# A decoder layer on one core: first-stage dummies, loads, small operations and products put at other places

## The chip, the cores and the metric

The kernel runs on one core of one Trainium2 chip. The metric is the time of one execution on the device in microseconds (us). The engines are named TensorE (PE, with its weight loads as PEld), VectorE (DVE), ScalarE (ACT), GpSimd (POOL) and SyncE (SP), whose queue issues most of the loads.

## What is computed

The reference is one layer of a conditioned decoder on 512 tokens of 1024 channels, in float32. Cut to what matters here:

```python
cs  = silu(c)                                   # c: one row of 1024
mod = cs @ w_ada + b_ada                        # six rows of 1024
shift1, scale1, gate1, shift2, scale2, gate2 = split(mod, 6)
h    = rmsnorm(x, norm1_g) * (1 + scale1) + shift1
proj = h @ w_in                                 # qa, ka, va, qd, kd, vd, ga, gd
out_a = sliding_window_attention(qa, ka, va, sinks)       # 8 heads, window 128
lam   = exp(sum(lp0 * lp1)) - exp(sum(lp2 * lp3)) + 0.2
out_d = rmsnorm(softmax_1 - lam * softmax_2 attention)    # 4 heads of two maps
merged = sigmoid(ga) * (out_a @ w_a) + sigmoid(gd) * (out_d @ w_d)
x = x + gate1 * (merged @ w_out)
x = x + gate2 * conv_ffn(rmsnorm(x, norm2_g) * (1 + scale2) + shift2)
return rmsnorm(x, final_g)
```

## The kernel before

Every product in float32 is made of three products in a faster format: a matrix is split in a high part and the low rest, and high x high, low x high and high x low are added up in PSUM. A split is a cast on ScalarE (the high part) and a subtraction on VectorE (the low part).

The change is in the **first stage**, which makes `h` (transposed, as `hTh` and `hTl`) and at the same time its products with the first 768 columns of `w_in` (`qa`, `ka`, `va`: six column blocks, in the six PSUM tiles `acc6`). It goes over eight row blocks k of 128 channels, the `GROUPS`:

- *Modulation.* The two rows `shift1` and `scale1` of block k need 1024 rows of `w_ada`, loaded as `adaw` (two loads of 512 KB, two buffers). `ac_ops` sums them up on VectorE, weighted by `cs`: eight steps in two chains, and one addition that ends in `ac`. `reduce_mod` sums `ac` over the partitions with two products on `ones` into `pa`, and `finish_mod` makes the two columns `mod` of it on VectorE.
- *h.* `x` comes in four token tiles `xn`. For each, `stat` squares it on ScalarE, and `rstd_start` and `rstd_end` make the root on VectorE and GpSimd. `normalise` scales the first 256 channels (VectorE), `turn` transposes block 0 on TensorE, `scale_x` scales the other channels (ScalarE), and `h_turn` transposes a later block. `h_tile` makes `hTh` and `hf` from the turned block and `mod` on ScalarE, and `h_low` makes `hTl` on VectorE.
- *Weights.* `w0_k` is loaded into one of four `raw` buffers; `split_hi` casts it on ScalarE (`w0h`), `split_lo` makes the low part `w0l` on VectorE in two parts (columns 0 to 511, 512 to 767).
- *Products.* `mm_k(k, part)` issues six products for each of three parts: `w0h` x `hTh`, `w0l` x `hTh`, `w0h` x `hTl`, that is all six PSUM tiles in one part before the next part.

Work runs one block ahead: while TensorE multiplies block k, VectorE sums the modulation of block k + 1. In this stage the order on VectorE, ScalarE and TensorE is that of the program text, written by hand (`manual_schedule`); the loads on SyncE's queue and whatever stands behind the stage in the text are placed by a planner, which may pull an instruction of the next stage in between.

Before the first product, TensorE has nothing to do for some time. `keep_warm(n)` gives it n products of the constants `ident` and `ones` into a PSUM tile that is overwritten later; each is two passes in the trace. In the code before there are 14 ahead of the first turn, and three behind each of the first three turns:

```python
    keep_warm(WARM)
    ac_ops(0, 0, KT)
    ...
    for t in range(NT):
        stat(t)
        if t:
            normalise(t - 1)
            turn(t - 1)
            keep_warm(3)
        if t == 1:
            finish_mod(0, reduce_mod(0))
```

Behind the stage, `evac_q` and `evac` move the six PSUM tiles out, and the products of the next weights start (`pq`, `pk`: heads of the second attention, units that `prefetch` loads and splits two ahead and that `fill` issues step by step). `ada_rows` sums the other four rows of the modulation on VectorE (`arow`) from loads `ra`, a step at a time between the products.

Of the kernel before, what the change touches and what calls it, by code (L numbers as in the profile page):

```python
# [8 lines left out]
F32 = mybir.dt.float32  # L9
# [26 lines left out]
NORM_LAG = 16  # L36
SWA_FILL = (2, 2, 5, 2, 2, 2, 2, 3)
DIFF_FILL = (3, 2, 4, 2)
WARM = 14
GROUPS = ((0,), (1,), (2,), (3,), (4,), (5,), (6,), (7,))  # L40
AC_CUT = 7
MOD_AT = 2
# [11 lines left out]
def kernel(  # L54
# [152 lines left out]
            )  # L207
        adaw[k] = aw

    load_ada(groups[0])  # L210
    for t in range(NT):
        nc.sync.dma_start(xn[:, t], xd[t * P : (t + 1) * P, :])
    for g in groups:
        if g[0]:
            load_ada(g)
        for k in g:
            r = raw_tile([P, 768], f"w0_{k}")
            nc.sync.dma_start(r, win[k * P : (k + 1) * P, 0:768])
            w0[k] = r
    nc.sync.dma_start(sink, swa_sinks[0].partition_broadcast(P))  # L220
    nc.sync.dma_start(
        lamv.rearrange("p a b -> p (a b)"), diff_lambda[0].rearrange("a b -> (a b)").partition_broadcast(P)
    )
    nc.sync.dma_start(crow[0:66, :], conv_w[0].rearrange("t (a p) -> (t a) p", p=P))
    nc.sync.dma_start(crow[66:88, :], conv_b[0].rearrange("(a p) -> a p", p=P))

    DONE = (0, 4, 2, 5, 1, 3)
    acc6 = {i: (fbank, sbank, vbank)[(0, 0, 1, 2, 1, 1)[i]](f"a{i}") for i in DONE}
# [5 lines left out]
    nc.vector.reciprocal(cs, cs)  # L234
    nc.vector.tensor_mul(cs, cs, pc8)
    pc = tbank("pc", (P, NR))
    nc.tensor.transpose(pc, rows, ident[:NR, :NR])
    cols = cpool.tile([P, NR], F32, name="cols")
    nc.vector.tensor_copy(cols, pc)
# [31 lines left out]
    def finish_mod(gi, pas):  # L271
        for k, pa in zip(groups[gi], pas):
            m = pp.tile([P, 16], F32, tag="mod", bufs=3, name=f"mod{k}")
            nc.vector.scalar_tensor_tensor(
                m[:, 0:1], pa[:, 0:1], bsc1[:, k : k + 1], n1g[:, k : k + 1], ALU.add, ALU.mult
            )
            nc.vector.tensor_add(m[:, 1:2], pa[:, 1:2], bsh[:, k : k + 1])
            mods[k] = m

    def w0_views(k):  # L280
        wh, wl = wts[k]
# [42 lines left out]
    def mm_k(k, part):  # L324
        wh, wl = wts[k]
        last = k == KT - 1
        if last and part == 2:
            return
        for i in DONE:
            for p in (1, 2) if last and part else (part,):  # L330
                lhs, rhs = ((wh, hTh), (wl, hTh), (wh, hTl))[p]
                nc.tensor.matmul(  # L332
                    acc6[i], lhs[:, i * P : (i + 1) * P], rhs[k], start=k == 0 and p == 0, stop=last and p == 2
                )


    def keep_warm(n):
        for i in range(n):
            nc.tensor.matmul(acc6[5][:, :P], ident, ones, start=True, stop=True)

    keep_warm(WARM)
    ac_ops(0, 0, KT)
    rst = pp.tile([P, NT], F32, name="rst")
    half = [None] * NT

# [17 lines left out]
    for t in range(NT):  # L363
        stat(t)
        if t:
            normalise(t - 1)
            turn(t - 1)
            keep_warm(3)
        if t == 1:
            finish_mod(0, reduce_mod(0))  # L370
    split_hi(0)
    normalise(NT - 1)
    turn(NT - 1)
    h_tile(0)
    split_lo(0, 0)
    split_lo(0, 1)
# [4 lines left out]
    for gi, g in enumerate(groups):  # L381
        nxt = groups[gi + 1] if gi + 1 < len(groups) else ()

        for k in nxt:
            split_hi(k)
        if gi == 0:
            for t in range(NT):
                scale_x(t)

        if nxt:  # L390
            ac_ops(gi + 1, 0, AC_CUT)
        h_low(g[0])
        if nxt:
            ac_ops(gi + 1, AC_CUT, KT)

        for k in g:
            if k == g[0] and len(nxt) == 1:
                h_turn(nxt[0])
            for part in range(3):
                if part == MOD_AT and k == g[-1] and nxt:  # L400
                    pas = reduce_mod(gi + 1)
                    split_lo(nxt[0], 0)
                    finish_mod(gi + 1, pas)
                    split_lo(nxt[0], 1)
                    for n in nxt[1:]:
                        split_lo(n, 0)
                        split_lo(n, 1)
                    for n in nxt:
                        if len(nxt) > 1:
                            h_turn(n)  # L410
                        h_tile(n)
                mm_k(k, part)
            if k == g[0]:
                for n in g[1:]:
                    h_low(n)
# [10 lines left out]
    def evac(hi, lo, src, scale=None):  # L426
        if scale is None:
            nc.scalar.copy(hi, src)
            nc.vector.tensor_sub(lo, src, hi.bitcast(F32))
        else:  # L430
            nc.scalar.activation(hi, src, AF.Copy, scale=scale)
            nc.vector.scalar_tensor_tensor(lo, src, scale, hi.bitcast(F32), ALU.mult, ALU.subtract)

    def evac_q(i):
        evac(qa[:, i, 0], qa[:, i, 1], acc6[i], qsc[:, i : i + 1])

    evac_q(0)
    evac(ka[:, 0], ka[:, 1], acc6[4])
    evac_q(2)
    vT = ap.tile([P, S], F32, tag="tmp", bufs=2, name="vaT")  # L440
    nc.scalar.copy(vT, acc6[5])
    evac_q(1)

    def turn_va():
        pv = tbank("pva")
# [6 lines left out]
    nc.tensor.transpose(pcv, crow, ident[:88, :88])  # L452
    cv = cpool.tile([P, P], F32, name="cv")
    nc.vector.tensor_copy(cv[:, :88], pcv)


    lp = cpool.tile([P, 2, 64], F32, name="lp")
    ls = cpool.tile([P, 2], F32, name="ls")
    nlam = cpool.tile([P, 1], F32, name="nlam")
    nc.vector.tensor_mul(lp, lamv[:, 0:4:2], lamv[:, 1:4:2])  # L460
    nc.vector.reduce_sum(ls, lp, axis=mybir.AxisListType.X)
    nc.scalar.activation(ls, ls, AF.Exp)
    nc.vector.tensor_sub(nlam, ls[:, 1:2], ls[:, 0:1])
    nc.vector.tensor_scalar_add(nlam, nlam, -LAM_INIT)
    nsink = cpool.tile([P, 8], F32, name="nsink")
    nc.vector.tensor_scalar_mul(nsink, sink, -1.0)


    def load_cols(src, col, name):
# [294 lines left out]
    def ada_rows():  # L764
        todo = [(idx, hf, k) for idx in range(4) for hf in range(2) for k in range(0, KT, 2)]
        r = ada_load(*todo[0])
        yield
        for (idx, hf, k), job in zip(todo, todo[1:] + [None]):
            nxt = ada_load(*job) if job else None
            if k == 0:  # L770
                ac = big.tile([P, S], F32, tag=("sq2", "g2b1")[hf], name=f"arow{idx}{hf}")
            with tc.high_priority(offset=HP // 2) if tick[0] > ADA_EASY else ExitStack():
                for a in range(2):
                    cc = cs[:, k + a : k + a + 1]
                    if k + a == 0:
                        nc.vector.tensor_scalar_mul(ac, r[:, a], cc)
                    else:
                        nc.vector.scalar_tensor_tensor(ac, r[:, a], cc, ac, ALU.mult, ALU.add)  # L778
            if k == KT - 2:
                after(ADA_LAG, lambda idx=idx, hf=hf, ac=ac: ada_spread(idx, hf, ac))  # L780
            r = nxt
            yield
# [46 lines left out]
    ada = ada_rows()  # L829
    add_head(0)  # L830
    add_head(1)
    fill(SWA_FILL[0])
    swa_scores(0, (0, 1))
    with tc.issue_after(pairs[0].last.ins):
# [982 lines left out]
```

## Time and profile before

| | us |
|---|---|
| median of three runs | 701.18 |
| the three runs | 700.99, 701.18, 702.16 |
| the profiled execution: its time | 702.35 |
| its span, first to last instruction | 700.5 |
| TensorE busy in the span | 682.6 |
| VectorE busy | 573.1 |
| ScalarE busy | 375.1 |
| mean granted TensorE clock | 0.995 |

Rows of the profile give the start and the duration in us, the engine, the line of the kernel (L332 is line 332), the operation, the tile that is written and those that are read, and in brackets the idle time of the engine just before and what ended it. Several like instructions in a row are one row with their count. TensorE's products overlap, so starts say more than durations.

### The profile page before, as it was taken

Reading aid. Unit: us, or ns where it says so; the run is one execution under the profiler, and the core shown is the slowest. Engines: PE = TensorE matmul, PEld = TensorE weight load, DVE = VectorE, ACT = ScalarE, POOL = GpSimd, SP = SyncE. Lnnn points to the kernel's source line nnn. Section 1 sums busy time; section 2 is a strip of 40 time slices with the busy share of each in tenths; the row PEclk is TensorE's granted clock in tenths of the full one; section 3 lists DMA queues with packets and bytes.
Section 4 is the critical chain, followed back from the end, with each engine's and each line's share of the span. In section 5 each row is a group of like instructions: output and inputs, shape, how many; then the busy total and the mean of one; then the engine's idle time right before and its main releaser. Section 6 shows DMA issues by size and latency. Waiting matters only on the chain.

```text
span 700.5 us, 11253 instructions
## 1 busy us (share of the span) xinstructions
PE 682.6 (97%) x4203; PEld 595.0 (85%) x4203; DVE 573.1 (82%) x1100; ACT 375.1 (54%) x666; POOL 82.4 (12%) x100
## 2 busy tenths in 40 slices
PE   6999999999999999999999999999999999999995
PEld 5777777777788888888889999999999999888884
DVE  5999886887985656663589999888888999979996
ACT  4646666454552333332468656655555666656664
POOL 3000000000001000000030111112111102540300
PEclk9999999999999999999999999999999999999998
DMA  9995454354535676239717788786889738997903
GB/s 313 289 273 159 149 152 151 98 173 121 140 102 160 207 232 185 91 99 281 251 39 144 151 200 199 174 209 184 209 213 217 173 129 219 191 198 196 166 1 120
DMA packets 115862, 121.81 MB, mean 174 GB/s; under 512 B 4383, under 2 KB 93280, under 8 KB 115808
## 3 DMA queue, kind: packets, MB, share of 16 engines
q1 hardware_dynamic: 96894, 95.09, 43.4%
q0 software_dynamic: 18720, 25.73, 22.0%
q8 instruction: 33, 0.54, 0.3%
q10 hardware_dynamic: 194, 0.28, 0.1%
q14 instruction: 21, 0.17, 0.1%
HBM read 118.97 MB, written 2.11 MB: 173 GB/s over the span
## 4 chain that ended last, share of the span: by engine, by line
PE 75%; DVE 13%; DMA 4%; ACT 4%; issue 2%; SPq 0%; POOL 0%; POOLq 0%; ACTq 0%
PE up L1152 26%; PE dc L1761 13%; DMA ra<-in_w_ada_dram 4%; PE a L332 3%; PE pgd L119 2%; PE oc L1208 2%; PE oc L1212 2%; PE pgd L121 2%; PE oc L1209 2%; PE pgd L120 2%; PE pga L119 2%; PE pga L121 2%; PE pga L120 2%; DVE arow L778 1%; DVE m_wlo L1097 1%
## 5 line engine op out<-in xcount | busy, mean ns | idle before, releaser
L1152 PE MATMUL up<-t,m_whi 128*128 128x256 f32 x528 | 96.2, 283 | 0.0
L1152 PEld LDWEIGHTS up<-t,m_whi 128*128 128x128 f32 x528 | 82.3, 192 | 0.0
L1152 PE MATMUL up<-t,m_wlo 128*128 128x256 f32 x264 | 74.7, 284 | 0.5 <-DVE m_wlo L1097 0.5
L1152 PE MATMUL up<-bh,p_wlo 128*128 128x256 f32 x232 | 65.6, 283 | 0.1
L1152 PE MATMUL up<-bh,p_whi 128*128 128x256 f32 x232 | 65.6, 283 | 0.0
L1152 PE MATMUL up<-bl,p_whi 128*128 128x256 f32 x232 | 65.6, 283 | 0.0
L778 DVE SCALAR_TENSOR_TENSOR arow<-ra,cs,arow 128x512 f32<-128x512 f32 x56 | 41.9, 749 | 21.0 <-DMA ra<-in_w_ada_dram 20.5
L1152 PEld LDWEIGHTS up<-t,m_wlo 128*128 128x128 f32 x264 | 50.6, 192 | 0.9 <-DVE m_wlo L1097 0.9
L1152 PEld LDWEIGHTS up<-bh,p_wlo 128*128 128x128 f32 x232 | 44.5, 192 | 0.3 <-DVE p_wlo L1097 0.3
L1152 PEld LDWEIGHTS up<-bl,p_whi 128*128 128x128 f32 x232 | 44.5, 192 | 0.0
L1152 PEld LDWEIGHTS up<-bh,p_whi 128*128 128x128 f32 x232 | 44.5, 192 | 0.0
L1065 POOL DMA_DIRECT2D s<-in_w_up_dram x21 | 27.0, 1360 | 143.1 <-DMA s<-in_w_up_dram 54.2
L1097 DVE TENSOR_TENSOR m_wlo<-s,m_whi 128x1024 fp32r<-128x1024 f32 x31 | 37.7, 1217 | 0.9 <-ACT m_whi L1093 0.9
L1093 ACT CAST m_whi<-s 128x1024 fp32r<-128x1024 f32 x31 | 32.4, 1047 | 9.6 <-DVE s L1087 6.2
L1152 PE MATMUL up<-t,p_whi 128*128 128x256 f32 x176 | 32.3, 284 | 0.5 <-DVE pairs L1192 0.5
L173 POOL TENSOR_TENSOR r<-ms,mhalf 128x1 f32<-128x1 f32 (+1 forms) x16 | 12.7, 796 | 133.1 <-DVE ms L171 74.1
L795 POOL DMA_DIRECT2D mod_rows<-row x8 | 5.1, 642 | 197.4 <-ACT row L794 197.4
L1152 PEld LDWEIGHTS up<-t,p_whi 128*128 128x128 f32 x176 | 27.4, 192 | 0.7 <-issue 0.7
L698 ACT ACTIVATE sd<-sd,dmx 128x128 f32<-128x128 f32 (+3 forms) x32 | 17.7, 557 | 19.0 <-DVE dmx L690 18.8
L1159 ACT ACTIVATE gT<-a,cv 128x512 f32<-128x512 f32 x22 | 17.7, 813 | 17.7 <-DVE a L1194 17.3
L1093 ACT CAST p_whi<-wa 128x1024 fp32r<-128x1024 f32 x18 | 18.7, 1041 | 12.0 <-PE up L1152 7.2
L1152 PE MATMUL up<-t,p_wlo 128*128 128x256 f32 x88 | 24.9, 283 | 0.0
(473 smaller groups left out, 2053.6 us busy)
## 6 DMA issues: line engine op xcount, KB each, us to landing
ra<-in_w_ada_dram SPq DMA_DIRECT2D x32, 512.0 KB, 3.9
wa<-in_w_up_dram SPq DMA_DIRECT2D x22, 512.0 KB, 4.0
s<-in_w_up_dram SPq DMA_DIRECT2D x21, 512.0 KB, 4.7
s<-in_w_up_dram POOLq DMA_DIRECT2D x21, 512.0 KB, 6.9
adaw<-in_w_ada_dram SPq DMA_DIRECT2D x16, 512.0 KB, 5.4
w<-in_w_in_dram SPq DMA_DIRECT2D x12, 512.0 KB, 3.9
a<-in_w_up_dram SPq DMA_DIRECT2D x11, 512.0 KB, 4.7
b<-in_w_down_dram SPq DMA_DIRECT2D x10, 512.0 KB, 3.8
```

What stands on the lines that cost most here:

```text
L119: nc.tensor.matmul(o, lh, rh, start=start, stop=False)
L120: nc.tensor.matmul(o, lh, rl, start=False, stop=False)
L121: nc.tensor.matmul(o, ll, rh, start=False, stop=stop)
L332: nc.tensor.matmul(acc6[i], lhs[:, i * P : (i + 1) * P], rhs[k], start=k == 0 and p == 0, stop=last and p == 2)
L698: exp = nc.scalar.activation(pm[m], pm[m], AF.Exp, bias=mx[:, m : m + 1], scale=slope, accum_out=lsum[:, m : m + 1])
L778: nc.vector.scalar_tensor_tensor(ac, r[:, a], cc, ac, ALU.mult, ALU.add)
L1065: nc.gpsimd.dma_start(dst, upblock(*blk), accum_op=ALU.add)
L1093: nc.scalar.copy(W[J, name][0], R[J, SRC[name]])
L1097: nc.vector.tensor_sub(lo, R[J, SRC[name]], hi.bitcast(F32))
L1152: nc.tensor.matmul(o[u], w[:, k, cu], b[:, k], start=name in ("p1", "m5", "p2") and k == 0 and x == 0, stop=k == 3 and x == 2, skip_group_ ...
L1159: nc.scalar.activation(grow(j), av[J][:, u], AF.Identity, bias=cv[:, 66 + j : 67 + j], scale=cv[:, 44 + j : 45 + j])
L1761: nc.tensor.matmul(bank2[u][:, sl], a[:, q, cu], b[:, q, sl], start=first_mm and x == 0, stop=last_mm and x == 2, skip_group_check=name no ...
```

## The change

- *Dummies:* 5 stand ahead of the transpose of `rows` (at about 4.8 us before), then 16 before and 8 behind the first reduction; behind the first three turns there are 3, 8 and 3, and 2 behind the last.
- *First sums of rows:* `reduce_mod(0)` is issued ahead of all turns; `finish_mod(0)` stays at its place on VectorE.
- *Loop:* `finish_mod` of the next block comes behind both parts of `split_lo`, no longer between them.
- *Products:* for all blocks but the last, `w0h` x `hTh` and `w0l` x `hTh` alternate tile by tile in part 0, and part 1 is empty. The order in the last block stays.
- *Loads:* the order of SyncE's first loads is written by hand. The loads of `sink`, `lamv` and `crow` come behind the last `adaw`.
- *Small operations:* the five on `lamv` and the one on `sink` are issued behind the last `h_low`.
- *Planner:* the splits of the first two head weights stay behind the last `mod` on VectorE, and the early `arow` sums behind the low part of `evac_q(1)`.

```diff
-WARM = 14
+WARM_EARLY = 5
+WARM = 24
...
-    load_ada(groups[0])
-    for t in range(NT):
-        nc.sync.dma_start(xn[:, t], xd[t * P : (t + 1) * P, :])
-    for g in groups:
-        if g[0]:
-            load_ada(g)
-        for k in g:
-            r = raw_tile([P, 768], f"w0_{k}")
-            nc.sync.dma_start(r, win[k * P : (k + 1) * P, 0:768])
-            w0[k] = r
-    (loads of sink, lamv, crow)
+    with tc.manual_schedule(engines={nc.sync.engine}):
+        load_ada(groups[0])
+        for t in range(NT):
+            nc.sync.dma_start(xn[:, t], xd[t * P : (t + 1) * P, :])
+        load_w0(0)
+        for k, ws in enumerate(((), (1,), (2, 3), (4, 5), (6,), (7,), (), ())):
+            if k:
+                load_ada(groups[k])
+            for n in ws:
+                load_w0(n)
+        (loads of sink, lamv, crow)
...
     pc = tbank("pc", (P, NR))
+    keep_warm(WARM_EARLY)
     nc.tensor.transpose(pc, rows, ident[:NR, :NR])
...
     def mm_k(k, part):
         wh, wl = wts[k]
         last = k == KT - 1
-        if last and part == 2:
+        if part == (2 if last else 1):
             return
         for i in DONE:
-            for p in (1, 2) if last and part else (part,):
+            for p in (1, 2) if last and part else (0, 1) if part == 0 and not last else (part,):
...
-    keep_warm(WARM)
+    keep_warm(WARM - 8)
     ac_ops(0, 0, KT)
+    pas = reduce_mod(0)
+    keep_warm(8)
...
             turn(t - 1)
-            keep_warm(3)
+            keep_warm((3, 8, 3)[t - 1])
         if t == 1:
-            finish_mod(0, reduce_mod(0))
+            finish_mod(0, pas)
     split_hi(0)
     normalise(NT - 1)
     turn(NT - 1)
+    keep_warm(2)
...
         h_low(g[0])
         if nxt:
             ac_ops(gi + 1, AC_CUT, KT)
+        else:
+            (lp, ls, its exponential on ScalarE, nsink, nlam: moved here)
...
                     pas = reduce_mod(gi + 1)
                     split_lo(nxt[0], 0)
-                    finish_mod(gi + 1, pas)
                     split_lo(nxt[0], 1)
+                    last_mod = finish_mod(gi + 1, pas)
...
-    evac_q(1)
+    read_q1 = evac_q(1)
...
-            with tc.high_priority(offset=HP // 2) if tick[0] > ADA_EASY else ExitStack():
+            with tc.high_priority(offset=HP // 2) if tick[0] > ADA_EASY else tc.issue_after(read_q1.ins):
...
     add_head(0)
     add_head(1)
+    with tc.issue_after(last_mod.ins):
+        prefetch()
     fill(SWA_FILL[0])
```

`issue_after(ins)` keeps the instructions of its block that run on the engine of `ins` behind `ins` in that engine's order; those on other engines and the loads are free.

## The prediction

> **What bounds the kernel now.** I read the page first: busy times, the 40 slices, the closing chain of waits.
>
> ```profile
> PE 682.6 (97%) x4203; PEld 595.0 (85%) x4203; DVE 573.1 (82%) x1100; ACT 375.1 (54%) x666; POOL 82.4 (12%) x100
> PE   6999999999999999999999999999999999999995
> PE 75%; DVE 13%; DMA 4%; ACT 4%; issue 2%; SPq 0%; POOL 0%; POOLq 0%; ACTq 0%
> ```
>
> TensorE is busy 97% of the span, and the only slices under 9 tenths are the first and the last. So TensorE's own queue sets the length, and what the change can win or lose lies in the first slices and in waits too short for a tenth to show. The change edits the first stage, which is what stands before the first `pq` product (about 60 us). I read that stretch in order of time. First the opening, up to the first product of input columns (L332):
>
> ```profile
> 2.40 0.24 PE L164 MATMUL pc<-ident,crow 8*128 8x8 f32 x1 [2.40 <-DMA crow<-in_c_dram]
> 4.80 0.27 PE L237 MATMUL pc<-ident,rows 25*128 25x25 f32 x1 [2.17 <-DMA rows<-in_diff_subln_g_dram]
> 5.00 6.14 PE L339 MATMUL a<-ones,ident 128*128 128x128 f32 x28
> 10.12 0.42 DVE L258 TENSOR_TENSOR ac<-ac,ac 128x256 f32<-128x256 f32 x1
> 11.73 0.37 DVE L356 TENSOR_SCALAR xn<-xn,rst 128x256 f32<-128x256 f32 x1
> 12.32 0.83 PE L339 MATMUL a<-ones,ident 128*128 128x128 f32 x6
> 12.99 0.50 PE L265 MATMUL pa<-ones,ac 128*128 128x1 f32 x4
> 13.53 0.22 DVE L274 SCALAR_TENSOR_TENSOR mod<-pa,cols 128x1 f32<-128x1 f32 x1 [1.44 <-PE pa L265]
> ...
> 14.64 0.47 PE L361 MATMUL xt<-ident,xn 128*128 128x128 f32 x1 [1.15 <-DVE ms L169]
> 14.91 1.49 PE L339 MATMUL a<-ones,ident 128*128 128x128 f32 x6
> 15.98 0.35 DVE L356 TENSOR_SCALAR xn<-xn,rst 128x256 f32<-128x256 f32 x1
> 16.25 0.68 DVE L304 TENSOR_TENSOR w0l<-w,w0h 128x512 fp32r<-128x512 f32 x1
> 16.41 1.42 PE L339 MATMUL a<-ones,ident 128*128 128x128 f32 x6
> 16.85 0.42 DVE L306 TENSOR_TENSOR w0l<-w,w0h 128x256 fp32r<-128x256 f32 x1
> 17.19 0.61 DVE L254 TENSOR_SCALAR ac<-adaw,cs 128x256 f32<-128x256 f32 x2
> 17.66 0.27 PE L361 MATMUL xt<-ident,xn 128*128 128x128 f32 x1
> 17.97 0.78 ACT L318 ACTIVATE hThA<-xt,mod 128x512 fp32r<-128x512 f32 x1 [3.50 <-PE xt L361]
> 18.80 1.42 PE L332 MATMUL a<-hThA,w0h 128*128 128x512 f32 x5 [0.43 <-ACT hThA L318]
> ```
>
> Columns are start, duration, engine, line, operation, output<-inputs, count. Three things are to be seen. The sum over rows of the first modulation weights is ready at 10.54 (10.12 + 0.42), but TensorE reaches its reduction `pa` only at 12.99, because it stands behind a turn of `xn` and three dummies; VectorE then waits 1.44 us for it, and the next `xn` scalings queue behind that wait. Second, six dummy passes take 0.83 us at 12.32 and 1.49 us at 14.91: (12.99 - 12.32) / 6 = 0.112 us a pass against (16.41 - 14.91) / 7 = 0.214 (six and a turn). The 28 passes from 5.00 hold 6.14, so nearly all of them ran at the slow pace too: it took some 5.8 us of steady work for the fast one. Third, the last `xn` tile is scaled by 16.33 (15.98 + 0.35), but its turn starts at 17.66, behind those slow dummies, and ScalarE's first `hThA` waits 3.50 us for it. The granted clock says the same:
>
> ```profile
> 10.00:15.00 5.00, 2.84 (x20) 2.56 (x19) 2.79 (x16) 4.25 (x8) 1.98 (x4) 0.92 1.09 372
> 15.00:20.00 5.00, 4.57 (x24) 4.15 (x24) 4.82 (x15) 2.03 (x4) 0.50 (x1) 0.74 1.11 364
> ```
>
> 0.92 and 0.74: half speed for about 0.8 us of the first and 2.6 of the second stretch, so about 14.2 to 17.6, after TensorE had stood idle for about 1.0 us behind 11.14 (5.00 + 6.14) and for 1.15 ahead of 14.64.
>
> Then the loop over the eight row blocks, k:
>
> ```profile
> 24.27 1.65 PE L332 MATMUL a<-hThA,w0h 128*128 128x512 f32 x6 [0.15 <-ACT hThA L318]
> 27.16 0.50 PE L265 MATMUL pa<-ones,ac 128*128 128x1 f32 x4
> 29.35 1.64 PE L332 MATMUL a<-hThA,w0h 128*128 128x512 f32 x6
> ...
> 34.66 1.65 PE L332 MATMUL a<-hThA,w0h 128*128 128x512 f32 x6
> ...
> 37.18 0.42 DVE L258 TENSOR_TENSOR ac<-ac,ac 128x256 f32<-128x256 f32 x1
> 37.52 0.69 DVE L304 TENSOR_TENSOR w0l<-w,w0h 128x512 fp32r<-128x512 f32 x1
> 37.75 0.58 PE L265 MATMUL pa<-ones,ac 128*128 128x1 f32 x4
> 38.37 0.22 DVE L274 SCALAR_TENSOR_TENSOR mod<-pa,cols 128x1 f32<-128x1 f32 x1 [0.16 <-PE pa L265]
> 38.57 0.42 DVE L306 TENSOR_TENSOR w0l<-w,w0h 128x256 fp32r<-128x256 f32 x1
> 38.90 0.61 DVE L254 TENSOR_SCALAR ac<-adaw,cs 128x256 f32<-128x256 f32 x2
> 40.03 1.64 PE L332 MATMUL a<-hThA,w0h 128*128 128x512 f32 x6
> ...
> 50.77 1.64 PE L332 MATMUL a<-hThB,w0h 128*128 128x512 f32 x6
> ...
> 55.86 1.65 PE L332 MATMUL a<-hThB,w0h 128*128 128x512 f32 x6
> ```
>
> From one k's first product to the next is 5.08 us once (24.27 to 29.35), and then 5.31, 5.37 and on average 5.36 (29.35 to 50.77 is 21.42 in four). The slow rounds are a ring of two engines. VectorE's sum `ac` starts at 37.18 and ends at 37.60; TensorE, done with its twelfth product, waits for it and does `pa` at 37.75; VectorE fills the latency with one part of `w0l` (37.52), runs dry, and takes `pa` up at 38.37 after 0.16 us of waiting, and only then does the other part of `w0l` (38.57) and the next seven `ac` steps. In the round of 5.08 `pa` (27.16) waits for nothing. Both engines are nearly full and each waits once for the other.
>
> **The change, part by part.**
>
> *Order in the loop.* Both parts of `w0l` now stand ahead of `mod`. From the first part to `mod` is 0.85 us now (37.52 to 38.37). The two parts back to back take 0.60 (16.25 to 16.85), and the second part to what follows 0.33 (38.57 to 38.90); the 0.33 was in the round before too. So VectorE's round goes from 5.36 to 5.36 - 0.85 + 0.60 = 5.11, or a little less without the small operations below. `pa` is then back before `mod` is reached: 0.85 after the first part against 0.93, so that wait goes. TensorE's own round without the wait is 5.08. What is late next is the two together, about 5.09: neither has more to give. Four rounds give 21.42 - 4 x 5.09 = 1.06; the sixth (50.77 to 55.86, no turns in it) loses the same wait of about 0.27. Sum: **-1.3 us**. `mod` comes 0.1 later after `ac`, so `hThA` does too; by the rows it is there at about 39.5 (38.37 + 0.22, a short `shift` step, 0.78) for products at 40.03, so 0.5 of slack covers that; without it the round would be 0.1 longer.
>
> *The products in another order* (high and low weight parts alternating per bank). The count stays at 18 a round and each has its own weight load as before, so I cost it at nothing. It asks for `w0l` at the second product instead of the seventh; in the loop that part is ready over 1 us early (38.57 + 0.42 = 38.99 against 40.03), at the start by 17.27 (16.85 + 0.42) against a second product near 18.
>
> *The opening.* `pa` of block 0 moves ahead of the turns, behind 5 and 16 dummies, and 8 + 3 + 8 + 3 dummies stand between it and the last turn. A dummy is two passes. The first five fill the idle stretch from 2.64 (2.40 + 0.24) to 4.80, so steady work starts there, and with the same 5.8 us the fast pace would come at about 8.4. Of the 32 passes from 5.0 on, 16 are then slow (3.4) and 16 fast (1.8): they end near 10.2, ahead of the sum at 10.54. `pa` then starts at 10.7 (0.15 behind the sum's end, as at 37.60 to 37.75) and takes 0.45. Then 44 passes at 0.112 are 4.93 and four turns some 0.5, so the last turn begins near 16.5, still behind its data: that was ready by 16.33 at the latest, and is earlier now without the 1.44 of waiting. `hThA` follows 0.31 behind (17.66 to 17.97): 16.8 for 17.97. I take **-1.1**. The next product block follows at the same distance, since ScalarE's queue (`hThA`, `hf`, a cast, four scalings of `xn`) sets it; VectorE's old times already suffice: `ac` of block 1 starts at 17.19 or earlier.
>
> With the clock at half for all 44 passes they take 9.4 us and `hThA` comes at 21.3, +3.3. These are the two ends. I take the fast one: the trace lost the clock after two pauses of 1.05 and 1.15 us within about 3.4, and the new order leaves one of at most about 0.7.
>
> The Trainium skill speaks against this part: "TensorE: Matmul & The Clock Gate", in "Why this matters for your kernels", asks only for no idle gaps over about 3 us, so pauses of 1.1 us would cost no clock and filling them would bring nothing. The trace disagrees: 0.74 granted behind such pauses. Part 1 of that page in the Trainium skill adds that the window in which activity is counted runs free, so the loss would vary from run to run; no single trace shows that.
>
> *Loads at fixed places.* They are issued in the order the trace already shows, except `sink`, `lamv` and the two `crow` loads, which go behind the last two blocks of modulation weights.
>
> ```profile
> 38.22 1.63 SPq L221 DMA_DIRECT2D lamv<-in_diff_lambda_dram  x1
> 39.90 0.38 SPq L224 DMA_DIRECT2D crow<-in_conv_w_dram  x1
> 42.51 1.02 SPq L205 DMA_DIRECT2D adaw<-in_w_ada_dram  x2
> 43.63 6.50 SPq L471 DMA_DIRECT2D w<-in_w_in_dram  x3
> ```
>
> That puts about 2.8 us of issue (1.63, and some 0.4 for each of three small ones) between 43.53 and the head weights now issued at 43.63, less the 0.75 by which three shorter rounds free the last slot sooner: they go 2.0 later. If their casts stand ahead of the last `hThB` in ScalarE's queue, as much of this as is not hidden stops TensorE: between 0 and 2.0 us. I take 0, as the moved loads are small and the transfers behind them start with emptier queues. The new ordering behind the last `mod` and behind `read_q1` binds only VectorE's instructions, which ran there already.
>
> *Small operations* (`lp`, `ls`, `nlam`, `nsink`) go behind the last `h_low`, where VectorE has no next block to sum: that hides them, and VectorE's rounds lose them. If `nlam` waits there for ScalarE's exponential, the splits of the head weights and the low parts of `qa` queue behind it, tenths of a us; TensorE then still has the twelve products of the last block.
>
> **The sum.** -1.3 - 1.1 = -2.4. The profiled execution took 702.35 (span 700.5 and 1.85 around it), so it would take 699.95. The median of the runs is 1.17 lower, and so is the spread between them (700.99 to 702.16): either the profile costs that much, then the sum gives 698.8, or those runs had a better opening, and then it stays near 699.9. I take 699.0. TensorE is busy in every later slice, so a shift at 58 us carries to the end. About 0.2%, 1.4 us, is what a measurement of this kernel can tell from no change.
>
> **The rivals.**
>
> *Only the loop gains* (18 in 100): the runs behind the median already have a good opening, or the pauses were not what slowed the dummies, so filling them brings nothing. By the rule of the Trainium skill's page the trace would have shown no slow passes at 14.91; it does. For the rival: the spread of 1.17. Against: the 3.50 us wait of `hThA` on the turn. 701.18 - 1.3 = 699.9, within 0.2%.
>
> *Only the opening gains* (10): the rounds stay near 5.36 because something else arrives as late, such as `hThA` behind the later `mod`, or the casts of late head weights hold ScalarE by over half of the 2.0. Against: the round of 5.08. 701.18 - 1.1 = 700.1, within 0.2%.
>
> *Slower* (10): the dummies themselves become the bound. They now stand on the path to the last turn, and each pass at half clock costs 0.1 more. 11 slow passes of the 44 eat the opening's gain, 24 the loop's as well; all of them cost 3.3 where 1.1 was gained: 701.18 + 3.3 - 1.3 = 703.2. For it: the trace shows 28 passes in a row at half clock, and a clock that fell after pauses of about 1 us. Against: from 2.6 us on there is hardly a pause left.
>
> *It does not do what it says*: the rest of the loads' order is the old one already, so that part alone would be 701.2; it is within the cases above.
>
> **How the numbers follow.** The forecast has 62 in 100, with its own range 697.6 to 699.8: -3.6 if the usual opening of the runs before has ten slow passes more than the profiled one (10 x 0.1, and the sum's 2.4), -1.4 with somewhat over half of each gain. The range of 8 in 10 reaches up over the two partial cases: 697.4 to 701.0, leaving out the slower one and the far tail of the forecast. Faster by over 0.2% (below 699.8) is the forecast's 62 and a few of the first partial case: 0.65; within 0.2% 0.25; slower 0.10.
>
> **What would show it.** Right: passes of 0.112 from about 8 us to the first product, granted clock 1.00 from 10 to 20, `pa` of block 0 near 10.7 without VectorE waiting, first product near 17.7, rounds of 5.1 and no wait of `mod` for `pa`; the first `pq` product near 57.7. Wrong: passes of 0.21 between `pa` and the last turn, rounds that stay above 5.3, ScalarE waiting for a head weight before the last `hThB`, or new waits of TensorE after 58 us.

## The result, and the profile after

The changed kernel took 700.33 us (median of 21 runs, 699.39 to 701.76); the kernel before, on the same chip, 701.80 (21 runs, 700.86 to 703.55). The ratio is 0.998, with a 95% interval of 0.9975 to 0.9986: 1.47 us faster, where the sum said 2.4 and the forecast, from the median given, 2.2. It lies inside the range (697.4 to 701.0) and half a microsecond above the likeliest case's own (up to 699.8). The profiled execution took 699.39 (span 697.5), the fastest of its 21; the profiled one of before (702.35) was half a microsecond slower than its median. So the two traces differ by 2.96 us, twice what the medians do, and must not be read as the typical pair.

The page of the changed kernel, busy times and TensorE's slices:

```profile
PE 684.4 (98%) x4247; PEld 597.7 (86%) x4247; DVE 572.8 (82%) x1100; ACT 375.4 (54%) x666; POOL 82.4 (12%) x100
PE   8999999999999999999999999999999999999995
```

The first slice rose from 6 tenths to 8; the 44 more matmul records are as many as 22 more dummies of two passes make. Busy time says nothing about gain here. The opening, in the timeline:

```profile
5.25 4.84 PE L247 MATMUL a<-ones,ident 128*128 128x128 f32 x32
9.49 0.43 DVE L271 TENSOR_TENSOR ac<-ac,ac 128x256 f32<-128x256 f32 x1
9.97 0.61 PE L278 MATMUL pa<-ones,ac 128*128 128x1 f32 x4
11.64 0.21 DVE L287 SCALAR_TENSOR_TENSOR mod<-pa,cols 128x1 f32<-128x1 f32 x1
...
13.20 1.95 PE L247 MATMUL a<-ones,ident 128*128 128x128 f32 x16
...
15.76 0.27 PE L372 MATMUL xt<-ident,xn 128*128 128x128 f32 x1
...
16.07 0.78 ACT L332 ACTIVATE hThA<-xt,mod 128x512 fp32r<-128x512 f32 x1 [1.90 <-PE xt L372]
16.90 0.50 PE L346 MATMUL a<-hThA,w0h 128*128 128x512 f32 x1
...
20.46 0.58 PE L278 MATMUL pa<-ones,ac 128*128 128x1 f32 x4 [0.54 <-DVE ac L271]
...
22.73 0.48 PE L346 MATMUL a<-hThA,w0h 128*128 128x512 f32 x1
```

`mod` waits for nothing, the dummies run at 0.12 a pass (16 in 1.95), and the first product starts at 16.90, 1.90 earlier than before. But the next block's first product is at 22.73, only 1.54 earlier: at 20.46 TensorE stands 0.54 us waiting for the sum `ac` of block 1, a row that had no counterpart before. The granted clock:

```profile
10.00:15.00 5.00, 5.00 (x46) 5.00 (x46) 3.18 (x17) 3.94 (x8) 2.52 (x4) 1.00 1.07 357
15.00:20.00 5.00, 4.92 (x30) 3.85 (x28) 4.79 (x13) 3.93 (x7) 0.00 (x0) 1.00 1.11 369
```

1.00 where it was 0.92 and 0.74. The rounds of the loop and the end of the stage:

```profile
27.83 0.49 PE L346 MATMUL a<-hThA,w0h 128*128 128x512 f32 x1
...
48.18 0.48 PE L346 MATMUL a<-hThB,w0h 128*128 128x512 f32 x1
...
53.22 1.66 PE L346 MATMUL a<-hThB,w0h 128*128 128x512 f32 x6
54.72 0.40 PE L346 MATMUL a<-hThB,w0l 128*128 128x512 f32 x1
55.23 0.50 PE L346 MATMUL a<-hTlB,w0h 128*128 128x512 f32 x1
...
57.88 0.39 PE L120 MATMUL pq<-hThA,w_h 128*128 128x512 f32 x1
```

Four rounds, 27.83 to 48.18, take 20.35 where 21.42 stood: 5.09 each. The last block, 53.22 to 57.88, takes 4.66; before it took 4.27, from 55.86 to this row:

```profile
60.13 0.39 PE L119 MATMUL pq<-hThA,w_h 128*128 128x512 f32 x1
```

VectorE shows why, first in the changed kernel and then in the one before:

```profile
51.90 1.22 DVE L117 TENSOR_TENSOR w_l<-w,w_h 128x1024 fp32r<-128x1024 f32 x1
53.19 0.25 DVE L478 COPY cv<-pcv 128x88 f32<-128x88 f32 x1
53.35 1.22 DVE L117 TENSOR_TENSOR w_l<-w,w_h 128x1024 fp32r<-128x1024 f32 x1
54.48 0.69 DVE L336 TENSOR_TENSOR hTlB<-hf,hThB 128x512 fp32r<-128x512 f32 x1
```

```profile
56.43 0.68 DVE L322 TENSOR_TENSOR hTlB<-hf,hThB 128x512 fp32r<-128x512 f32 x1
...
57.09 1.21 DVE L116 TENSOR_TENSOR w_l<-w,w_h 128x1024 fp32r<-128x1024 f32 x1
```

Two splits of head weights now stand ahead of `hTlB`, where the second stood behind it before. TensorE needs `hTlB` at 54.95 (54.72 and one spacing of 0.23) and starts on it at 55.23; the first product behind the pause costs another 0.1 (the next one follows 0.33 later, not 0.23). Up to the first `pq` product the trace has gained 2.25 us (60.13 to 57.88): 1.54, then 1.07 in the four rounds and 0.03 in the other two, less 0.39.

### The profile page after: what moved, and what is told of

Its sections match the earlier page's. It is cut to its first block, busy times and chain, and to the rows that moved or that the text cites. A ratio compares the mean times of both kernels' runs of the same rounds, so it can differ in the third digit from the quotient of the medians.

```text
span 697.5 us, 11341 instructions
## 1 busy us (share of the span) xinstructions
PE 684.4 (98%) x4247; PEld 597.7 (86%) x4247; DVE 572.8 (82%) x1100; ACT 375.4 (54%) x666; POOL 82.4 (12%) x100
## 4 chain that ended last, share of the span: by engine, by line
PE 82%; DVE 10%; DMA 3%; ACT 3%; issue 2%; SPq 0%; POOLq 0%; POOL 0%; ACTq 0%; DVEq 0%
PE up L1166 26%; PE dc L1775 13%; PE a L346 4%; PE pgd L120 2%; PE oc L1222 2%; PE oc L1223 2%; PE pgd L122 2%; PE oc L1226 2%; PE pgd L121 2%; DMA adaw<-in_w_ada_dram 2%; PE pga L120 2%; PE pga L122 2%; PE pga L121 2%; DVE m_wlo L1111 1%; DMA ra<-in_w_ada_dram 1%
```

## The experiments

Each was timed against the kernel before on its own chip, and the chips differ by about 1 us, so ratios are compared and not times; "changed" is the changed kernel (0.9980). Starts of products are read from the timelines. The order of the loads and the place of the small operations were not undone by themselves.

**One part undone at a time.** First the order in the loop:

```diff
-                    split_lo(nxt[0], 1)
                     last_mod = finish_mod(gi + 1, pas)
+                    split_lo(nxt[0], 1)
```

> The changed kernel with one part undone: mod of the next block is made between the two parts of w0l again. Theory (the ring of VectorE and TensorE sets the rounds, and this order breaks it): rounds of 5.09 us go back to 5.3, the wait of mod for pa returns, about 1.1 us of the 1.5 us gain are lost, -0.4 against the kernel before. Rival (the alternating products, which stay in, make the rounds shorter): rounds stay at 5.09 and the gain stays at 1.5.

Measured: 702.45 us, ratio 0.9998 (0.9986 to 1.0011). The rounds are 5.34, 5.34, 5.35, 5.34 and 5.22 again. Nearly the whole measured gain goes with this one exchange of two instructions: 0.0018, 1.3 us, with an error of 0.9. In the trace the six rounds behind block 1 take 1.2 us more than in the changed kernel. The exchange also moves `last_mod`, to which the early fetch is pinned: the second split falls behind `hTlB` again, and the last block takes 4.29.

The opening (old dummies, and `pa` of block 0 behind the first turn):

```diff
-    keep_warm(WARM_EARLY)
+    keep_warm(0)
...
-    keep_warm(WARM - 8)
+    keep_warm(14)
     ac_ops(0, 0, KT)
-    pas = reduce_mod(0)
-    keep_warm(8)
...
-            keep_warm((3, 8, 3)[t - 1])
+            keep_warm(3)
...
-            finish_mod(0, pas)
+            finish_mod(0, reduce_mod(0))
...
-    keep_warm(2)
```

> The changed kernel with the opening undone: 14 dummies ahead, three behind each of the first three turns, the first reduction behind the first turn. Theory (slow passes and VectorE's wait for pa delay the first product): the first product comes about 1 us later than in the changed kernel, the granted clock falls below 1 between 10 and 20 us, and the gain shrinks to 0.5. Rival (pauses of about 1 us cost no clock, and the opening is set by the loads of x): the first product stays, and so does the gain of 1.5.

Measured: 702.10, ratio 0.9986 (0.9977 to 0.9995). The first product is at 18.89, block 1's at 24.36, the granted clock 0.95 and 0.71 in the two stretches; rounds of 5.04 to 5.17. Undoing the opening costs 0.4 us of the time, within the errors of nothing, although this trace has the slow passes.

The order of the products (all high parts, then all low parts):

```diff
-            for p in (1, 2) if last and part else (0, 1) if part == 0 and not last else (part,):
+            for p in (1, 2) if last and part else (part,):
```

> The changed kernel with the products in the old order: all six of the high weights, then all six of the low. Theory (18 products at the same pitch either way): rounds of 5.09 and the gain of 1.5 stay, within 0.2 us. Rival (two products in a row into one PSUM tile run faster): the twelve products take longer by 0.1 us or more a round, and half a us or more of the gain is lost.

Measured: 701.78, ratio 0.9985 (0.9972 to 0.9999). The undisturbed rounds are 5.06 to 5.10, as in the changed kernel, so the order is worth nothing that can be seen. Two rounds took 5.56 and 5.95, and the longer one has its reason in these rows, VectorE's first and then TensorE's:

```profile
32.89 0.62 DVE L267 TENSOR_SCALAR ac<-adaw,cs 128x256 f32<-128x256 f32 x2 [0.76 <-DMA adaw<-in_w_ada_dram]
```

```profile
37.09 0.58 PE L278 MATMUL pa<-ones,ac 128*128 128x1 f32 x4 [0.66 <-DVE ac L271]
```

A load of modulation weights came late, the sum behind it too, and TensorE stood. This is nothing the order of products could cause; it became the question of the later runs.

The dummies alone (`pa` first stays, old numbers of dummies):

```diff
-    keep_warm(WARM_EARLY)
+    keep_warm(0)
...
-    keep_warm(WARM - 8)
+    keep_warm(14)
...
-    keep_warm(8)
...
-            keep_warm((3, 8, 3)[t - 1])
+            keep_warm(3)
...
-    keep_warm(2)
```

> The changed kernel with the old dummies (14 ahead, three behind each of the first three turns), but with the first reduction still ahead of all turns. Tells the two halves of the opening apart. If VectorE's wait for pa is the whole loss, the last xn is ready as early as in the changed kernel and fewer dummies stand in the way: hThA 0.4 us earlier than there, gain 1.5 to 1.9. If the clock is what counts, the pauses between the turns return, passes run at 0.214 us, and hThA comes 0.8 later than in the changed kernel: gain 0.7.

Measured: 701.90, ratio 0.9981 (0.9972 to 0.9990), the changed kernel's own.

```profile
16.73 0.50 PE L346 MATMUL a<-hThA,w0h 128*128 128x512 f32 x1 [0.43 <-ACT hThA L332]
20.66 0.58 PE L278 MATMUL pa<-ones,ac 128*128 128x1 f32 x4 [0.92 <-DVE ac L271]
```

The first product is no later than with all the dummies (16.73), and the wait for block 1's sum is longer for it (0.92). What the opening gains in this trace comes with the move of `pa`; the additional dummies add nothing that can be seen.

**No dummies at all.**

```diff
-    keep_warm(WARM_EARLY)
+    keep_warm(0)
...
-    keep_warm(WARM - 8)
...
-    keep_warm(8)
...
-            keep_warm((3, 8, 3)[t - 1])
...
-    keep_warm(2)
```

> The changed kernel without a single product on constants: `pa` of block 0 first, then turns, then the real products. By the prediction's step (steady work for some 5.8 us before the fast pace) the first block's products run at half pace for about 5.8 us: 0.46 us each for 0.23, some 12 products, 2.9 us lost, of which 0.5 to 0.9 was waiting for the next block's sum anyway: first `pq` 2.0 to 2.4 later, time +2 us against the changed kernel (ratio 1.001). Rival: products on constants are needless altogether, since the turns and `pa` warm the clock or nothing needs warming: granted clock near 1.00 from 17 us on, first `pq` at 58, ratio 0.998.

Measured: 702.36, ratio 0.9993 (0.9983 to 1.0004).

```profile
16.79 0.80 PE L346 MATMUL a<-hThA,w0h 128*128 128x512 f32 x1
17.39 0.63 PE L346 MATMUL a<-hThA,w0l 128*128 128x512 f32 x1
17.81 0.63 PE L346 MATMUL a<-hThA,w0h 128*128 128x512 f32 x1
...
19.00 0.40 PE L346 MATMUL a<-hThA,w0l 128*128 128x512 f32 x1
```

The first products are spaced by some 0.43 instead of 0.23, but only five of them, not twelve, and block 1's sum would have been waited for anyway: block 1's product comes at 22.85, no later than in the traces with all dummies (22.73 to 23.23). The first `pq` product is at 58.22, 0.34 behind the changed kernel, of which 0.2 falls in one long round (5.30). So the theory's 2.0 to 2.4 us missed, and up to the end of the stage the rival, that dummies are needless, nearly holds, though the first products were slow. The time is 0.9 us above the changed kernel's all the same; where that went is not settled. Between 60 and 160 us this trace lost 1.3 us against that of the kernel before, more than any other but one.

**The pins.** The first sums of rows and the early fetch of head weights are set free again:

```diff
-            ... else tc.issue_after(read_q1.ins):
+            ... else ExitStack():
...
-    with tc.issue_after(last_mod.ins):
-        prefetch()
```

> The changed kernel without the two pins: the first sums of rows `arow` may go anywhere, and the head weights are fetched where the first product asks. VectorE's order then has two `arow` ahead of the first low part of `qa`, and one head weight's split behind `hTlB` (it was ahead). Theory: the pins are worth little: the last block gets back to 4.3 us (-0.37), the `arow` steps of 1.2 us ahead of `qa` delay the evacuation but TensorE has the `pq` products meanwhile; ratio 0.9975 to 0.9985. Rival: the first `arow` waits for its load, `qa` and the first scores behind it, TensorE waits after 58 us, ratio 0.9990 or more.

Measured: 701.15, ratio 0.9989 (0.9980 to 0.9998). The last block is 4.29, as expected. But the trace shows the largest wait of all, on a load:

```profile
48.76 0.62 DVE L267 TENSOR_SCALAR ac<-adaw,cs 128x256 f32<-128x256 f32 x2 [1.26 <-DMA adaw<-in_w_ada_dram]
```

```profile
53.97 0.58 PE L278 MATMUL pa<-ones,ac 128*128 128x1 f32 x4 [2.17 <-DVE ac L271]
```

The loads are issued in the changed kernel's order, so this late load is not put down to the pins; a late load is also in the trace with the products undone. The time lies 0.6 us above the changed kernel's, just under the rival's 0.9990, and is not told from no difference.

**The last block.** The early fetch is cut in two, the second split behind the last low part:

```diff
-    with tc.issue_after(last_mod.ins):
-        prefetch()
+    for ins in (last_mod.ins, low.ins):
+        with tc.issue_after(ins):
+            load, run = units.pop(0)
+            loaded.append((load(), run))
```

> The changed kernel, with the early prefetch of the head weights cut in two: the first split stays behind the last `mod`, the second goes behind the last low part `hTlB`. Theory: in the changed kernel the second split (1.2 us on VectorE) stands ahead of `hTlB`, TensorE waits 0.5 us for it, and the last block takes 4.66 us up to the first `pq` product instead of 4.27. With the split behind it that stretch is 4.3, the first `pq` comes near 57.5, and the time falls by 0.3 us (ratio 0.9975). Rival: the second split is then late for `pq`, and TensorE waits there instead: same time, a wait on the low weights in front of `pq`.

Measured: 701.29, ratio 0.9980 (0.9971 to 0.9989). The last block takes 4.29 instead of 4.66, as expected; the 0.3 us don't appear in the time, whose error is larger. This trace again had a late load (0.59 us, in a round of 5.78) and one more long round (5.36).

**Late loads in the loop.** The weights of blocks 1 to 7 are not loaded, in the changed kernel and in the one before:

```diff
         k, m = g[0], len(g)
+        if k:
+            adaw[k] = adaw[0]
+            return
```

> The changed kernel with the modulation weights of blocks 1 to 7 left unloaded: their sums run as before, on block 0's weights (that part of the output is then another). It takes 7 MB of loads out of the first 45 us. Theory: at the pace of 5.09 us a round the loads are what comes late next; in four of seven traces of the changed loop a sum `ac` waited for its `adaw` and cost TensorE 0.4 to 0.9 us in a round. Without them every round is 5.04 to 5.10, the first `pq` product comes at 57.9 or earlier, and the time is 0.4 to 0.8 us below the changed kernel (ratio 0.9970). Block 0 to block 1 stays near 5.7, since VectorE's own work (splits, then eight `ac` steps) sets that, not the load. Rival: those late loads are rare in the timed runs; then the ratio stays at 0.998 and the loss is after the first stage.

> The kernel before with the same loads left out (and the first sums of rows kept behind the reads of the input product, where they stood anyway). Theory: its rounds of 5.3 to 5.4 are the ring of `pa` and `mod`, so they stay; the loads never were late at that pace; it takes what before takes (ratio 0.9995 to 1.0), and the pair without loads differs by 2.0 us or more, nearly the forecast's sum. Rival: the pair differs by 1.5 as the two kernels do.

Measured, changed: 700.74, ratio 0.9985 (0.9976 to 0.9994). Five rounds are 5.03 to 5.14 without a late one, the sixth is 4.72; block 1 comes at 22.68 and the first `pq` product at 57.75, as the theory had it. The time is not lower, though, and the ratio is within its error of the rival's 0.998. In the trace 0.7 us go at the very end, where the last store takes 4.09 us from its issue (694.86) to the end of the span, against 3.38 in the changed kernel. The kernel before without the loads loses as much there (4.10), and none of the twelve traces with the loads does (3.36 to 3.38); why, no trace shows. So these two times carry something that the loads in the loop did not cause, and what the late loads cost in the timed runs stays open. (The expectation's "four of seven" counted a round of 5.30 in which no row shows a wait for a load; it was three of seven.)

Measured, before: 704.85, ratio 1.0041 (1.0029 to 1.0053). Its rounds stayed at 5.33 to 5.42, as expected, but the planner, finding the load free, put a head weight's split ahead of the last sum `ac`, which cost a round of 6.02, and more waits came after 60 us. The pair is not comparable, and its difference of 4 us proves nothing. The expectation failed by the experiment's own making.

**Sums behind the loads of the next stage.** In several traces the gain up to 58 us shrank again by 100 us. TensorE in the kernel with the old dummies, between 80 and 97 us:

```profile
82.69 0.96 PE L127 MATMUL sw<-ka,qa 64*128 64x256 f32 x11 [0.47 <-DVE outal L451]
96.14 0.97 PE L127 MATMUL sw<-ka,qa 64*128 64x256 f32 x11 [0.39 <-DVE outal L451]
```

And on VectorE, ahead of `outal`, in the same kernel:

```profile
80.70 0.49 DVE L786 TENSOR_SCALAR arow<-ra,cs 128x512 f32<-128x512 f32 x1 [1.88 <-DMA ra<-in_w_ada_dram]
...
94.74 0.75 DVE L788 SCALAR_TENSOR_TENSOR arow<-ra,cs,arow 128x512 f32<-128x512 f32 x1 [1.66 <-DMA ra<-in_w_ada_dram]
```

So two sums were put behind `outal`, in the changed kernel and in the one before, all else as it was:

```diff
+            late = outs.get({(0, 1, 0): 0, (0, 1, 4): 1}.get((idx, hf, k)))
-            with tc.high_priority(...) if tick[0] > ADA_EASY else ...:
+            with tc.issue_after(late.ins) if late else tc.high_priority(...) if tick[0] > ADA_EASY else ...:
```

> The changed kernel, with two sums of rows put behind other work on VectorE: the first row of the fifth and of the seventh pair of weight rows of the second modulation (`arow<-ra`, which in the trace waited 1.76 and 1.21 us for their loads ahead of the low part `outal` of a finished head pair) now go behind that `outal`. Nothing else moves. Theory: of the 2.0 to 2.2 us that the first stage gains up to the first `pq` product, 0.4 to 0.9 is lost again between 80 and 97 us in most executions, because `outal`, and with it TensorE, waits behind a sum whose load lands at its own pace. Then this kernel is 0.4 to 0.9 us faster than the changed one (ratio to before 0.9965 to 0.9975), and no wait of TensorE on `outal` is in the trace. Rival: the loss lies in the first stage of the executions that are not profiled; then it takes what the changed kernel takes, 0.9980 of before.

> The kernel before, with the same two sums put behind `outal`. Theory: before, the waits of `outal` are hardly on TensorE's path (0.2 us lost there in the one trace), so this takes about what before takes, ratio 0.9995 (-0.3 us), and the difference to its changed partner is then the whole gain of the first stage, 1.9 to 2.2 us. Rival: both kernels win alike from the new place, so that the difference between the partners stays near 1.5 us: then the waits for `ra` are not where the gain went.

Measured: changed 699.91, ratio 0.9957 (0.9944 to 0.9969); before 700.66, ratio 0.9975 (0.9964 to 0.9987). No wait of TensorE on `outal` is left in either trace. The rival was right: both win, the kernel before by 1.75 us, and the pair differs by 0.0018 with an error as large, no more than the two kernels do. So nothing shows that the waits for `ra` eat the change's gain in particular: they cost both. In the old kernel this edit alone gains no less than the whole change does (0.9975 and 0.9980).

**Both mended places together:**

> The changed kernel with both mended places: two sums of rows behind `outal`, and the second head weight's split behind `hTlB`. Theory: the gains add, 1.5 us by the first and 0.3 by the second: last block 4.3, no wait on `outal`, ratio 0.9953. Rival: where the load of `ra` was the bound, work that comes earlier waits for it anyway: ratio 0.9957 as with the first alone.

Measured: 699.31, ratio 0.9965 (0.9953 to 0.9976). First `pq` product at 57.63, last block 4.29, no wait on `outal`. By the intervals it isn't told from the kernel with the two sums alone (0.9957); these two are the fastest versions, some 1 us below the changed kernel or more.

## Why the prediction was right, and where it was not

**What bounds the kernel.** Right: the loop's ring was the thing to break, and breaking it is nearly the whole measured gain.

**Order in the loop** (-1.3). The four rounds gave 1.07 in the profiled execution, as worked out, and undoing that part alone costs 1.3 us. The sixth round went from 5.09 to 5.04, not to 4.82. There TensorE waits for `hThB`, and ScalarE starts `hThB` 0.40 us behind the end of `mod`. Without the modulation loads it started 0.10 behind, and that round took 4.72. The rows of `mod` and `hThB`, in the changed kernel and then without the loads:

```profile
51.84 0.15 DVE L290 TENSOR_TENSOR mod<-pa,cols 128x1 f32<-128x1 f32 x1
52.39 0.78 ACT L332 ACTIVATE hThB<-xt,mod 128x512 fp32r<-128x512 f32 x1 [2.19 <-DVE mod L290]
```

```profile
51.70 0.15 DVE L293 TENSOR_TENSOR mod<-pa,cols 128x1 f32<-128x1 f32 x1
51.95 0.78 ACT L335 ACTIVATE hThB<-xt,mod 128x512 fp32r<-128x512 f32 x1 [2.43 <-DVE mod L293]
```

What holds ScalarE for the 0.3 no trace shows; and without the loads the 0.3 were lost again in front of `hTlB` (last block 4.95).

The step that was missing: "neither has more to give" named two engines, and forgot the loads. A pair of modulation loads was issued 7.15 us before its use in the kernel before (42.51 to 49.66) and 6.57 before it now (40.24 to 46.81):

```profile
49.66 0.61 DVE L254 TENSOR_SCALAR ac<-adaw,cs 128x256 f32<-128x256 f32 x2
```

```profile
46.81 0.60 DVE L267 TENSOR_SCALAR ac<-adaw,cs 128x256 f32<-128x256 f32 x2
```

The trace of before already had landings that would be too late at this pace. This is the second load of an earlier pair, the time to its landing, and its first use:

```profile
26.79 1.34 SPq L205 DMA_DIRECT2D adaw<-in_w_ada_dram  x1
```

```profile
adaw<-in_w_ada_dram SPq DMA_DIRECT2D x1, 512.0 KB, 6.5
```

```profile
33.56 0.61 DVE L254 TENSOR_SCALAR ac<-adaw,cs 128x256 f32<-128x256 f32 x2
```

It landed at 33.3, 6.9 after the pair's first issue (26.36) and 0.3 ahead of its use; 6.57 would not have been enough. So the slack is gone: of nine traces with the new loop and its loads, four have a round of 5.59 to 7.41 in which `ac` waits 0.45 to 1.26 us for `adaw`; of three with the old loop (before, the loop undone, and before with two sums moved) none. The rounds' excess over 5.09 in the nine is 0.6 us on average: 0 in three, 0.1, 0.2, 0.5, 1.0, 1.4 and 2.5 in the rest. Rounds of 5.23 to 5.56 in four of them are counted in it though their rows show no wait for a load. The spread of the timed runs says nothing for or against: without the loads ten of eleven runs lie within 0.9 us, but all eleven within 2.3, and the 21 of the changed kernel within 2.4.

**Loads at fixed places** (0). Mis-ordered. I had the head weights 2.0 us later; the first one in fact went 7 us earlier, ahead of the last modulation weights:

```profile
36.55 1.72 SPq L483 DMA_DIRECT2D w<-in_w_in_dram  x1
40.24 1.00 SPq L206 DMA_DIRECT2D adaw<-in_w_ada_dram  x2
```

The first load of the last pair took this long to land, before, changed, and in the kernel without pins:

```profile
adaw<-in_w_ada_dram SPq DMA_DIRECT2D x1, 512.0 KB, 3.7
```

```profile
adaw<-in_w_ada_dram SPq DMA_DIRECT2D x1, 512.0 KB, 4.1
```

```profile
adaw<-in_w_ada_dram SPq DMA_DIRECT2D x1, 512.0 KB, 6.3
```

That fits: a transfer of 512 KB now stands in front of it. With the loop undone, where the order of the loads stays, it was 5.4, so the slower landing does not need the shorter round. The head weight's place was not tried by itself, and it can have to do only with the two late loads of the last pair; the other two late ones, at about 33 us, were issued before it. I also had it that the new ordering "binds only VectorE's instructions, which ran there already"; the second split stands ahead of `hTlB` now, and this cost 0.39 us in the last block, shown by moving it back (4.29).

**Products in another order** (0). Right.

**The opening** (-1.1 for `hThA`). It came at 16.07 where 16.8 was forecast, 0.6 of the difference being a first modulation load that landed earlier in that execution (first `ac` step at 6.47 for 7.10). The step that failed is the one behind it: "the next product block follows at the same distance", because "VectorE's old times already suffice". They don't: its two splits, the eight `ac` steps with `hTlA` between them and the addition end at 20.31, and the earlier TensorE comes, the longer it waits there (0.54, and 0.92 with the old dummies). And the base was one draw of two. The kernel before, its opening untouched, showed this in the run with two sums moved:

```profile
10.00:15.00 5.00, 2.30 (x20) 2.03 (x19) 2.31 (x16) 4.18 (x8) 2.23 (x4) 1.00 1.08 369
15.00:20.00 5.00, 4.57 (x28) 3.76 (x27) 4.86 (x14) 3.38 (x6) 0.36 (x1) 1.00 1.09 359
```

Full clock, although TensorE paused for 1.55 and 1.15 us, no less than the 1.0 and 1.15 of the other trace; first product at 17.45, block 1's at 23.49 instead of 24.27. Of four traces with the old opening two lost clock (block 1's product at 24.27 and 24.36) and two didn't (23.49, and 23.16 without the loads). In the two that lost it the half clock adds up to the same 3.4 us (0.8 and 2.6 by the clocks of 0.92 and 0.74; 0.5 and 2.9 by 0.95 and 0.71). The eight with the new opening and all loads, or with `pa` first and the old dummies, all had 1.00 and block 1's product at 22.73 to 23.23. So at block 1 the opening is worth 0.3 to 1.6 us, 1.1 between the averages with all loads (24.04 of three, 22.95 of eight): the size forecast, but as a mean over two kinds of execution, and the run with the opening undone found 0.4 of it in the time.

The advice of the Trainium skill in "TensorE: Matmul & The Clock Gate", "Why this matters for your kernels", to leave TensorE no idle gap over about 3 us, was not enough here: 0.74 stands behind pauses of 1.0 and 1.15 us. The free-running window of Part 1 of that page of the Trainium skill fits: the same code, paused alike, lost clock in one execution and not in another. What I made of it was too firm, "the trace lost the clock after two pauses": the pauses were a condition, not a cause that always acts, and filling them with more dummies brought nothing once `pa` stood first.

**Small operations** (0). `nlam` stands at 57.21, behind a wait of `qa` for ScalarE that was there before (0.77 us; 0.48 before), and itself waits for nothing. Right.

**The sum.** Put together from averages, the first stage gains 1.1 (opening) and 1.1 (rounds), and loses 0.4 (last block) and 0.6 (late loads): -1.2, against a measured -1.47 with an error of 0.4. The forecast's -2.4 had the two gains, 0.2 too much for the sixth round, and nothing for the two losses. That the late loads and the last block are the missing microsecond is a sum over traces, and the times don't confirm it: without the loads the ratio was no lower than the changed kernel's (0.9985), nor with the split moved back (0.9980). So this cause is argued and not shown. In the range itself there is a slip: ten slow passes of 0.1 and the sum's 2.4 make 3.4, not 3.6, so the lower end would have been 697.8.

"A shift at 58 us carries to the end" holds from 205 us on, where the distances between the traces stay constant within 0.1 up to the last stage. Between 60 and 160 us an execution wins or loses up to 1.3 (the kernel before without the loads 2.2), a part of it by when its `ra` loads land, as the waits on `outal` show; the rest was not traced.

Of the rivals, "only the loop gains" comes nearest: 1.3 us of the 1.47. "Slower" had the dummies on the path at half clock; none of these passes was slow after 8 us.

## What to carry to other kernels

When a ring of two engines is broken, price the third member before the gain is booked: how long before its use is each load issued, and how does that compare with the longest landing, not the median, that the trace shows? Here a landing of 6.5 us stood in the trace before the change, next to a time to use that was about to fall to 6.57 from the pair's first issue. Judge an opening by the second block's first product, not by the first's: what comes sooner than the next sum is only waited for. And before a stage's gain is compared with a median, look at how far the profiled executions stand from theirs; here the traces said 2.96 and the runs 1.47.

## What the runs showed of the hardware

The granted clock of a cold TensorE reads 1.00 while its passes take twice as long: without dummies the stretch 15 to 20 us shows 1.00, with the products 0.43 and then 0.23 us apart.

```profile
15.00:20.00 5.00, 4.58 (x16) 3.53 (x16) 4.88 (x13) 4.04 (x7) 0.00 (x0) 1.00 1.11 370
```

The column tells of a loss behind a warm start (0.74, 0.71), not of the warm-up itself. And the warm-up did not ask for unbroken work: the fast pace was there at about 19 us, after `pa` and eight turns, spread over 10.1 to 16.8 with pauses of 0.4 to 0.9 us, and some 2 us of products. That is about 6 us of busy time in 9, where steady dummies took some 5.8.

The other surprise is what a load's time to landing does: the modulation loads of the loop, 512 KB each, landed from 3.7 us behind their issue (the last pair's first, in the kernel before) to 7.5 (its second, in the kernel without pins). A round that leaves 6.57 us from a pair's first issue to its use was late in some executions and not in others.
